# Gathers that wait for a row buffer alone, and inner units moved around the gate products

## The chip, the cores and the metric

The kernel runs on one core of a Trainium2 chip. Its time is the device time of one execution in microseconds (us). Engines are named as in the profile: PE multiplies matrices, PEld loads its weights, DVE works on vectors, ACT evaluates functions, POOL issues the gathers, SP issues most other transfers. Each engine works through its own list of instructions in the order in which the list was built; it waits for semaphores of the others.

## The reference, cut to what matters

One layer of a diffusion transformer over 512 tokens of 2048 numbers: modulation, a retention mixer and an mLSTM mixer, their merge, and then the part that this change touches, a product-key expert layer:

```python
qh = (tb @ w_query).reshape(P_BLOCK, P_HEADS, 2, P_DQ // 2)
s = einsum('thpd,hpkd->thpk', qh, sub_keys)            # 128 + 128 keys per head
sv, si = top_k(s, 16)                                  # per token, head and half
best_s, best_j = top_k(all 16 x 16 sums, 16)           # -> 16 experts of 16384 per head
eid, g = ids of the best, softmax(best_s)
act = gelu(einsum('thkd,td->thk', expert_down[eid], tb))
out = einsum('thk,thkd->td', g * act, expert_up[eid])
```

There are 8 heads, so each token picks 128 expert rows of 2048 numbers, once from expert_down and once from expert_up.

## The kernel before, in words

The kernel computes the expert layer in two ways at once. For 352 of the 512 tokens it is dense: it multiplies all 16384 experts (128 tiles of 128, the inner units, name `hid`) with the tokens, applies Gelu, multiplies with a mostly empty matrix of gates (`gd`, `gt`) and multiplies the result (`hh`) with expert_up (`pac`, `upp`). For the other 160 tokens (128 and 32) it gathers: POOL fetches, for one slot of every token, one row of expert_down or expert_up per partition, 1 MB in all, into a row buffer (`row`). A DVE instruction then forms the scalar product with the token (L1309, function `down`) or adds the weighted row to the result (L1318, function `up`). There are 320 such gathers, 160 of each kind, in a fixed order of slots: slots 0 to 15 of the first 128 belong to head 0, 16 to 31 to head 1, and so on.

Weights arrive as fp32 blocks of 512 KB (`raw`, seven buffers). ACT rounds each to a high part (L228), DVE subtracts to get the low part (L229, called a split here; 770 in all), and PE makes three products of each pair of blocks (L238 to L240). A split pair lives in one of three `ws` buffers, so DVE can be at most three blocks ahead of PE.

The expert layer runs in these stages, told apart here by the count of splits:

- **A, selection** (function `select`): for each of 8 heads PE makes the query products of two halves and the scores (`sc`), and DVE picks the 16 best per half (`top16`, 128-wide), then the 16 best of 256 sums, and finds the ids and gates (`pick`). `pick` of head h writes 16 columns of `eid`. Between the heads PE makes dense tiles that are spilled to memory (`hs`).
- **B, gates** (function `gating`): the selections are transposed, DVE builds one-hot rows (`o`, L1227 to L1231), PE multiplies them (`gp`, L1243) in 88 steps, the results go out in 11 blocks (`gd`). The dense tiles 18 to 55 are spread among these steps: NE_PRE of them ahead, NE_POST behind, the others between.
- **C and D, experts** (function `experts`): for 16 groups of 8 tiles, the second multiplication and the rest of the dense tiles. C is the part up to the 596th split, D the part behind it, up to the closing stage E.

The instructions are written down in the order of the program, and a scheduler of the kernel language then lays them out on each engine: an instruction moves forward to where its inputs and its buffer are free, if the engine has nothing more urgent. The calls `gather(n)` in the dense work spread the 320 slots evenly over stages B to D (SPAN counts the units). A gather, and with it the DVE instruction on its row, is therefore placed by three things: its slot's ids are there, a row buffer is free, and, before the change, the last PE product written ahead of it has been made (`self.last`, `add_manual_dep` in function `rows`). The three row buffers are shared: in stage A one holds the keys (`keys`) and one the selections (`sel`); the third is free once the transposed tokens (`xn`) are done with at the start of A.

Of the kernel before, what the change touches and what calls it, by code (L numbers as in the profile page):

```python
# [12 lines left out]
AF = mybir.ActivationFunctionType  # L13
OP = mybir.AluOpType
AX = mybir.AxisListType
PACE = mybir.DependencyInfo(mybir.DependencyClass.Sync, mybir.DependencyReason.DATA)
PSUM = bass.MemoryType.PSUM
DRAM = bass.MemoryType.DRAM

# [2 lines left out]
KT = D // P  # L22
# [127 lines left out]
X1_BUFS = 5  # L150
NPA = 4
NE_HEAD, NE_SEL = 16, 18
NE_PRE, NE_POST = 1, 2
OT, OB = 8, 2

GX = 32
# [1 line left out]
ND = T - G_  # L158
# [24 lines left out]
class K:  # L183
# [64 lines left out]
    def tjob(self, srcs, targets, nk=KT, order=range(8), one=False):  # L248

        n, last = 0, len(targets) - 1  # L250
        for u, src in enumerate(srcs):
            w = self.weight(src)
            for k8 in order if u else range(8):
                if n == self.LATE:
                    self.flush()
                if n in self.STEPS and self.mixing:
                    next(self.mixing, None)
                c = slice(k8 * P, (k8 + 1) * P)
                for t, (ps, rhs) in enumerate(targets):
                    self.last = self.mm3(ps, (w[:, 0, c], w[:, 1, c]), rhs(u * 8 + k8),  # L260
                                         n == 0 and not (one and t), n == nk - 1 and not (one and t < last))
                n += 1

# [1001 lines left out]
    def spill_steps(self, tiles):  # L1265
        for i in tiles:
            ps = self.ps("hid")
            for u in range(2):
                w = self.weight(self.a["dn"][i, u])
                for k8 in range(8):  # L1270
                    kt = u * 8 + k8
                    c = slice(k8 * P, (k8 + 1) * P)
                    self.last = self.mm3(ps[:, :ND], (w[:, 0, c], w[:, 1, c]), self.HD[kt], kt == 0, kt == KT - 1)
                    if k8 == 7:
                        self.gather(HIDG // 2)
                    if kt < KT - 1:
                        yield
            f = self.d0.tile([P, ND], F32, name="hf", bufs=4)
            self.S.activation(f, ps[:, :ND], AF.Gelu)
            t = self.dp.tile([P, ND], F32, name=f"hs{i}")  # L1280
            self.SY.dma_start(t, f)
            self.HS.append(t)
            yield
# [6 lines left out]
    def gatherer(self):  # L1290

        a, V, S, G, d0 = self.a, self.V, self.S, self.G, self.d0

        dots = [d0.tile([P, n], F32, name=f"dots{n}") for n in (P, GX)]
        wts = [d0.tile([P, n], F32, name=f"wts{n}") for n in (P, GX)]
        eid = [self.eid[0].rearrange("p h k -> p (h k)"), self.eid[1]]
        gacc = [d0.tile([P, D], F32, name=f"gacc{i}", tag=f"h2n{i}") for i in range(2)]
        fold = d0.tile([P, GX], F32, name="fold")
        V.tensor_reduce(fold, self.ident.rearrange("p (q t) -> p t q", t=GX), AX.X, OP.add)

        def rows(src, i, s_):
            r = self.rowbuf([P, D], "row")
            g = G.indirect_dma_start(out=r, out_offset=None, in_=src,  # L1303
                                     in_offset=bass.IndirectOffsetOnAxis(ap=eid[i][:, s_:s_ + 1], axis=0))
            self.tc.add_manual_dep(g.ins, self.last.ins.name, PACE, reason="pace of the gathers")
            return r

        def down(i, s_, r):
            V.scalar_tensor_tensor(r, r, 1.0, self.h2n[i], op0=OP.mult, op1=OP.mult, accum_out=dots[i][:, s_:s_ + 1])  # L1309
            if s_ == dots[i].shape[1] - 1:  # L1310
                S.activation(wts[i], dots[i], AF.Gelu)
                V.tensor_mul(wts[i], wts[i], self.gates[i])

        def up(i, s_, r):
            if s_ == 0:
                V.tensor_scalar(gacc[i], r, wts[i][:, 0:1], None, OP.mult)
            else:
                V.scalar_tensor_tensor(gacc[i], r, wts[i][:, s_:s_ + 1], gacc[i], op0=OP.mult, op1=OP.add)  # L1318

        slots = [(f, w, i, s_) for f, w in ((down, a["dnr"]), (up, a["up"])) for i, n in enumerate((P, GX)) for s_ in range(n)]  # L1320
        NS = len(slots)
        late = []
        done = 0

        def gather(n):

            nonlocal done
            done += n
            while slots and NS - len(slots) < NS * done // SPAN:
                row()  # L1330

        def row():

            if slots:
                f, w, i, s_ = slots.pop(0)
                late.append((f, i, s_, rows(w, i, s_)))
            if len(late) > LAG or not slots:
                f, *x = late.pop(0)
                f(*x)

        self.slots, self.late, self.row, self.gather, self.gacc, self.fold = slots, late, row, gather, gacc, fold

    def experts(self, d2):
        a, V, S, TE, SY, G, d0 = self.a, self.V, self.S, self.TE, self.SY, self.G, self.d0
# [21 lines left out]
        def end0():  # L1366
            nonlocal xg, xh, sqg
            while slots or late:
                row()
            t = d2.tile([P, 2, T], F32, name="xs", tag="gt", bufs=2)  # L1370
            xh, sqg = t[:, 0].rearrange("p (k t) -> p k t", k=KT), t[:, 1]
            xg = self.rowbuf([P, KT, P], "xg")
            SY.dma_start(xg, self.X1[:, :, :P].rearrange("k p t -> p k t"))
            SY.dma_start(xh, self.X1[:, :, P:G_].rearrange("k p t -> p k t"))
# [92 lines left out]
        for g in range(NG):  # L1467
            for i in range(len(hs), min(GRP * (g + 1) + FORE, P)):
                if g == NG - 1 and i % GRP == GRP - 3:
                    end0()  # L1470
                    end1()
                elif g == NG - 1 and i % GRP == GRP - 1:
                    self.todo += [end3, end2]
                hs.append(tile(i))
            hh = hs[GRP * g:GRP * (g + 1)]

            def part(w, q, d_, ps, js):

                own = d_ >= NPA
                for j in js:  # L1480
                    c = slice(j * 256 + d_ % 2 * P, j * 256 + (d_ % 2 + 1) * P)
                    i = 4 * q + j
                    self.last = self.mm3(ps[:, :ND], (w[:, 0, c], w[:, 1, c]), (hh[i][:, 0], hh[i][:, 1]),
                                         i == 0 and (own or g == 0), i == GRP - 1 and (own or g == NG - 1))

            for q in range(GRP // 4):
                ws = [self.weight(a["upt"][g, u, q]) for u in range(NPA // 2)]
                for js in (range(3), (3,)) if g == NG - 1 and q == GRP // 4 - 1 else (range(4),):
                    for d_ in range(NPA):
                        part(ws[d_ // 2], q, d_, pac[d_], js)  # L1490
                gather((UP if (g + 1) * GRP > NE else UP0) * NPA // 2 * 4 // GRP)
            if g == NG - 1:
                for d_ in range(NPA):
                    x2[d_] = d0.tile([P, ND], F32, name="hf", bufs=4)
                    final(d_, pac[d_], xd[:, d_])
            for u in range(8):
                if g == NG - 1 and u in END:
                    (end4, end5)[END.index(u)]()
                if u >= NPA // 2:
                    ds = (2 * u, 2 * u + 1)  # L1500
                    pss = [self.ps("upp") for _ in ds]
                    for q in range(GRP // 4):
                        w = self.weight(a["upt"][g, u, q])
                        for d_, ps in zip(ds, pss):
                            part(w, q, d_, ps, range(4))
                            if q < GRP // 4 - 1:
                                continue
                            if g == 0:
                                V.tensor_copy(x2[d_], ps[:, :ND])
                            elif g < NG - 1:  # L1510
                                V.tensor_add(x2[d_], x2[d_], ps[:, :ND])
                            else:
                                final(d_, ps, x2[d_])
                    gather(UP if (g + 1) * GRP > NE else UP0)
        r = self.r2[:, :ND]
# [18 lines left out]
```

## Time and profile before

Three runs took 4078.6, 4090.9 and 4102.6 us (median 4090.9). The profiled execution took 4096.7 us, its span is 4094.9 us, and its mean granted PE clock 0.981.

| engine | busy us | share | instructions |
|---|---|---|---|
| PE | 3955.3 | 97% | 22470 |
| DVE | 2855.7 | 70% | 4448 |
| ACT | 1325.9 | 32% | 1823 |
| POOL | 500.4 | 12% | 328 |

986 MB are moved, 241 GB/s on the mean. The span is best read by the stages, since DVE and the transfers are at 0.2 to 0.5 of their capacity in the middle of the kernel and at 0.8 to 0.95 in most of its second half, where all the gathers are. In a stretch's row the columns are its length, the busy time of each engine with its count of instructions, the granted PE clock, the busy share of the DMA engines, and GB/s.

### The profile page before, as it was taken

The numbers are of one execution on the slowest core, as the hardware profiler recorded it, in microseconds if no ns is written. First come the engines' busy times: TensorE is split into PE (matmuls) and PEld (weight loads), VectorE is DVE, ScalarE is ACT, GpSimd is POOL, SyncE is SP. The second block draws the span as 40 slices with busy tenths as digits, with TensorE's granted clock in tenths as the row PEclk, the third lists the DMA queues.
The fourth block names the chain that finished last, engine by engine and source line by source line (L and its number), as shares of the span: only waits on it lengthen the run. The fifth ranks groups of instructions, "written<-read, shape, count | busy, mean of one in ns | idle before, by whom it ended". The sixth has DMA issues, their size and how long they took to land.

```text
span 4094.9 us, 56734 instructions
## 1 busy us (share of the span) xinstructions
PE 3955.3 (97%) x22470; PEld 3577.1 (87%) x22470; DVE 2855.7 (70%) x4448; ACT 1325.9 (32%) x1823; POOL 500.4 (12%) x328
## 2 busy tenths in 40 slices
PE   7999999999999999899999998999999999999998
PEld 4788887777788888799989998999999999999998
DVE  7852237677733443488888987888888787888886
ACT  3322124344422222433333333323233332333333
POOL 0000000000000000000001112222222332233320
PEclk7999999999999999999999999999999999999998
DMA  8522237667733444433358898999898898988993
GB/s 298 215 75 85 70 102 256 233 207 245 261 127 112 140 150 149 152 106 109 102 188 303 308 328 342 373 339 371 337 348 342 342 351 326 354 343 345 357 340 102
DMA packets 305723, 986.21 MB, mean 241 GB/s; under 512 B 32944, under 2 KB 106928, under 8 KB 264368
## 3 DMA queue, kind: packets, MB, share of 16 engines
q1 hardware_dynamic: 257072, 642.82, 45.3%
q0 software_dynamic: 46080, 335.56, 21.1%
q10 hardware_dynamic: 2304, 4.20, 0.3%
q8 instruction: 176, 2.88, 0.3%
q14 instruction: 91, 0.75, 0.0%
HBM read 918.87 MB, written 63.57 MB: 240 GB/s over the span
## 4 chain that ended last, share of the span: by engine, by line
PE 56%; DMA 18%; issue 13%; DVE 9%; POOL 2%; ACT 1%; SPq 0%; POOLq 0%; DVEq 0%; ACTq 0%
PE px L240 10%; PE px L239 10%; PE px L238 10%; DMA row<-in_dnr,eid 6%; DMA row<-in_up,eid 6%; DVE ws L229 3%; PE upp L238 2%; PE upp L240 2%; PE upp L239 2%; PE va L238 2%; PE va L239 2%; PE va L240 2%; PE hid L238 2%; PE hid L240 2%; PE hid L239 2%
## 5 line engine op out<-in xcount | busy, mean ns | idle before, releaser
L228 ACT CAST ws<-raw 128x1024 fp32r<-128x1024 f32 x770 | 806.8, 1049 | 1742.2 <-PE px L240 565.3
L229 DVE TENSOR_TENSOR ws<-raw,ws 128x1024 fp32r<-128x1024 f32 x770 | 938.3, 1221 | 563.5 <-ACT ws L228 562.7
L240 PE MATMUL hid<-h,ws 128*128 128x352 f32 x2048 | 662.1, 323 | 24.3 <-DVE ws L229 24.1
L238 PE MATMUL hid<-h,ws 128*128 128x352 f32 x2048 | 677.3, 331 | 0.0
L239 PE MATMUL hid<-h,ws 128*128 128x352 f32 x2048 | 661.8, 323 | 0.0
L1303 POOL DMA_INDIRECT row<-in_dnr,eid x128 | 190.8, 1491 | 2735.1 <-DVE o L1228 2060.1
L238 PE MATMUL upp<-hh,ws 128*128 128x352 f32 x1536 | 500.0, 325 | 0.0
L240 PE MATMUL upp<-hh,ws 128*128 128x352 f32 x1536 | 493.0, 321 | 6.0 <-DVE ws L229 6.0
L239 PE MATMUL upp<-hh,ws 128*128 128x352 f32 x1536 | 494.2, 322 | 0.0
L1309 DVE SCALAR_TENSOR_TENSOR row<-row,h2n 128x2048 f32<-128x2048 f32 x160 | 366.1, 2290 | 123.4 <-DMA row<-in_dnr,eid 97.0
L1318 DVE SCALAR_TENSOR_TENSOR gacc<-row,wts,gacc 128x2048 f32<-128x2048 f32 x158 | 371.2, 2350 | 113.8 <-DMA row<-in_up,eid 95.2
L238 PE MATMUL px<-hhi,ws 128*128 128x512 f32 x1024 | 413.7, 404 | 0.0
L240 PEld LDWEIGHTS hid<-h,ws 128*128 128x128 f32 x2048 | 387.6, 189 | 29.4 <-DVE ws L229 29.1
L240 PE MATMUL px<-hhi,ws 128*128 128x512 f32 x1024 | 408.6, 399 | 0.0
L239 PE MATMUL px<-hlo,ws 128*128 128x512 f32 x1024 | 406.4, 397 | 0.0
L239 PEld LDWEIGHTS hid<-h,ws 128*128 128x128 f32 x2048 | 392.2, 192 | 0.0
L238 PEld LDWEIGHTS hid<-h,ws 128*128 128x128 f32 x2048 | 387.7, 189 | 0.0
L240 PEld LDWEIGHTS upp<-hh,ws 128*128 128x128 f32 x1536 | 289.0, 188 | 7.1 <-DVE ws L229 7.1
L239 PEld LDWEIGHTS upp<-hh,ws 128*128 128x128 f32 x1536 | 292.4, 190 | 0.0
L238 PEld LDWEIGHTS upp<-hh,ws 128*128 128x128 f32 x1536 | 288.6, 188 | 0.0
L1303 POOL DMA_INDIRECT row<-in_up,eid x128 | 207.3, 1619 | 460.1 <-PE hid L240 183.9
L240 PEld LDWEIGHTS px<-hhi,ws 128*128 128x128 f32 x1024 | 192.7, 188 | 48.0 <-issue 2.9
(451 smaller groups left out, 6496.3 us busy)
## 6 DMA issues: line engine op xcount, KB each, us to landing
raw<-in_dn SPq DMA_DIRECT2D x256, 512.0 KB, 5.7
raw<-in_upt SPq DMA_DIRECT2D x256, 512.0 KB, 6.0
raw<-in_wada_r SPq DMA_DIRECT2D x160, 512.0 KB, 4.6
raw<-in_wt SPq DMA_DIRECT2D x130, 512.0 KB, 3.6
gd<-sg SPq DMA_DIRECT2D x11, 2048.0 KB, 13.0
gt<-gd SPq DMA_DIRECT2D x32, 704.0 KB, 7.9
raw<-in_wada_s SPq DMA_DIRECT2D x32, 512.0 KB, 6.0
raw<-in_wn SPq DMA_DIRECT2D x32, 512.0 KB, 3.5
```

Source lines behind the costliest of these rows:

```text
L228: self.S.copy(w[:, 0], r)
L229: self.V.tensor_sub(w[:, 1], r, w[:, 0].bitcast(F32))
L238: mm(out, lhsT=l[0], rhs=r[0], start=start, stop=False)
L239: mm(out, lhsT=l[0], rhs=r[1], start=False, stop=False)
L240: return mm(out, lhsT=l[1], rhs=r[0], start=False, stop=stop)
L1303: g = G.indirect_dma_start(out=r, out_offset=None, in_=src, in_offset=bass.IndirectOffsetOnAxis(ap=eid[i][:, s_:s_ + 1], axis=0))
L1309: V.scalar_tensor_tensor(r, r, 1.0, self.h2n[i], op0=OP.mult, op1=OP.mult, accum_out=dots[i][:, s_:s_ + 1])
L1318: V.scalar_tensor_tensor(gacc[i], r, wts[i][:, s_:s_ + 1], gacc[i], op0=OP.mult, op1=OP.add)
```

## The change

`rows` issues the gather and no longer makes it wait for a PE product. With that the assignments to `self.last`, which served nothing else, and the constant PACE go. NE_PRE goes from 1 to 2 and NE_POST from 2 to 4, so that 32 tiles of inner units instead of 35 lie between the gate products.

```diff
-NE_PRE, NE_POST = 1, 2
+NE_PRE, NE_POST = 2, 4
...
         def rows(src, i, s_):
             r = self.rowbuf([P, D], "row")
-            g = G.indirect_dma_start(out=r, out_offset=None, in_=src,
-                                     in_offset=bass.IndirectOffsetOnAxis(ap=eid[i][:, s_:s_ + 1], axis=0))
-            self.tc.add_manual_dep(g.ins, self.last.ins.name, PACE, reason="pace of the gathers")
+            G.indirect_dma_start(out=r, out_offset=None, in_=src,
+                                 in_offset=bass.IndirectOffsetOnAxis(ap=eid[i][:, s_:s_ + 1], axis=0))
             return r
...
-                    self.last = self.mm3(ps[:, :ND], (w[:, 0, c], w[:, 1, c]), self.HD[kt], kt == 0, kt == KT - 1)
+                    self.mm3(ps[:, :ND], (w[:, 0, c], w[:, 1, c]), self.HD[kt], kt == 0, kt == KT - 1)
```

The change has a second part that the diff doesn't show: without the PE product the scheduler lays the gathers and the instructions on their rows elsewhere. Counted in the built order of DVE, with the splits as the measure of the place:

| stage | splits | row instructions before | after |
|---|---|---|---|
| A | 238 to 297 | 0 | 42 |
| B | 298 to 373 | 41 | 68 |
| C | 374 to 596 | 164 | 210 |
| D | 597 to 759 | 115 | 0 |

The first 40 gathers of the new order all use one row buffer, that of `xn`, and each waits for the DVE instruction on the row before; the next four use two buffers, and all later ones three.

**DVE, stage A, the turn from head 0 to head 1, before.** `sel`, `ef`, `eid` and `ex` end the pick of a head, `ws` is a split, the MAX rows begin the 16 best of the next scores.

```order
1189 L1150 CAST ex<-ef 32x16
1190 L229 TENSOR_TENSOR ws<-raw,ws 128x1024
1191 L1182 MAX sv<-score 128x8 x2
1192 L1183 MAX_INDEX si<-sv,score 128x8 x2
1193 L1184 MATCH_REPLACE score<-sv,score 128x128 x2
```

There the pick is followed by a split and at once by the next head's scores. The same place after; `row,dots` are the products of a gathered row:

```order
1189 L1149 CAST ex<-ef 32x16
1190 L228 TENSOR_TENSOR ws<-raw,ws 128x1024
1191 L1307 SCALAR_TENSOR_TENSOR row,dots_15685<-row,h2n_11758 128x2048 x2
1192 L1181 MAX sv<-score 128x8 x2
1193 L1182 MAX_INDEX si<-sv,score 128x8 x2
1194 L228 TENSOR_TENSOR ws<-raw,ws 128x1024
```

Two row products have come in between, side by side. After, a few rows on, behind two of the four blocks of scores:

```order
1202 L1185 MAX_INDEX si<-sv,score 128x8 x2
1203 L1307 SCALAR_TENSOR_TENSOR row,dots_15685<-row,h2n_11758 128x2048
1204 L228 TENSOR_TENSOR ws<-raw,ws 128x1024
1205 L1307 SCALAR_TENSOR_TENSOR row,dots_15685<-row,h2n_11758 128x2048
1206 L1181 MAX sv<-score 128x8 x2
```

Two more stand here with a split between them. After, the end of the next head's pick:

```order
1251 L1307 SCALAR_TENSOR_TENSOR row,dots_15685<-row,h2n_11758 128x2048
1252 L1145 TENSOR_TENSOR sel<-gt,sm 128x4x16
1253 L1148 SCALAR_TENSOR_TENSOR ef<-sel 128x16
1254 L1148 SCALAR_TENSOR_TENSOR ef<-sel 32x16
1255 L1149 CAST eid<-ef 128x16
1256 L1149 CAST ex<-ef 32x16
1257 L228 TENSOR_TENSOR ws<-raw,ws 128x1024
1258 L1307 SCALAR_TENSOR_TENSOR row,dots_15685<-row,h2n_11758 128x2048 x2
```

So six row products have come into each head, at the same places of every head: two side by side behind the pick, one behind the first two blocks of scores, one a split later, and two in the pick (1243, ahead of the CAST of `bf`, and 1251).

**DVE, stage C, near split 430, before.** `acc` adds a product of the second multiplication.

```order
2137 L1511 TENSOR_TENSOR acc<-acc,upp 128x352
2138 L229 TENSOR_TENSOR ws<-raw,ws 128x1024
2139 L1309 SCALAR_TENSOR_TENSOR row,dots_15685<-row,h2n_11758 128x2048
2140 L229 TENSOR_TENSOR ws<-raw,ws 128x1024
2141 L1511 TENSOR_TENSOR acc<-acc,upp 128x352
2142 L1309 SCALAR_TENSOR_TENSOR row,dots_15685<-row,h2n_11758 128x2048
2143 L1511 TENSOR_TENSOR acc<-acc,upp 128x352
2144 L229 TENSOR_TENSOR ws<-raw,ws 128x1024 x2
```

With three row products to four splits. After:

```order
2203 L1307 SCALAR_TENSOR_TENSOR row,dots_15686<-row,h2n_11759 128x2048
2204 L228 TENSOR_TENSOR ws<-raw,ws 128x1024
2205 L1307 SCALAR_TENSOR_TENSOR row,dots_15686<-row,h2n_11759 128x2048
2206 L228 TENSOR_TENSOR ws<-raw,ws 128x1024
2207 L1509 TENSOR_TENSOR acc<-acc,upp 128x352 x2
2208 L1307 SCALAR_TENSOR_TENSOR row,dots_15686<-row,h2n_11759 128x2048
2209 L228 TENSOR_TENSOR ws<-raw,ws 128x1024
```

Now a row product stands behind every split.

## Rows read from the trace of the kernel before

**Rows 1.** Stretches: stages A, B, C, D and E.

```profile
core 0: us, PE busy (x) PEld busy (x) DVE busy (x) ACT busy (x) POOL busy (x), PEclk, DMA share, GB/s
...
1776.00:2088.00 312.00, 310.65 (x2157) 309.93 (x2156) 259.35 (x881) 102.38 (x124) 0.00 (x0) 1.00 0.36 111
2088.00:2480.00 392.00, 364.48 (x2887) 350.64 (x2886) 323.54 (x394) 145.48 (x208) 64.48 (x41) 0.97 0.86 298
2480.00:3369.80 889.80, 867.69 (x5349) 861.23 (x5348) 747.62 (x791) 279.62 (x339) 241.65 (x165) 0.99 0.92 351
3369.80:4021.00 651.20, 634.35 (x3916) 631.58 (x3915) 529.42 (x456) 202.63 (x249) 189.84 (x115) 0.99 0.88 333
4021.00:4095.00 74.00, 58.77 (x368) 57.97 (x366) 49.28 (x107) 22.36 (x34) 0.00 (x0) 0.90 0.32 100
```

**Rows 2.** The same stretches, DVE's splits (L229) alone.

```profile
1776.00:2088.00 312.00, 72.54 (x60) 1.00 0.36 111
2088.00:2480.00 392.00, 92.69 (x76) 0.97 0.86 298
2480.00:3369.80 889.80, 270.01 (x223) 0.99 0.92 351
3369.80:4021.00 651.20, 197.13 (x163) 0.99 0.88 333
```

**Rows 3.** Waits, 1776 to 2080 us: us in total, times, longest.

```profile
DVE sv L1182 <- ACT score L1115: 38.6, 13, 3.4
...
DVE ws L229 <- ACT ws L228: 12.7, 7, 1.9
```

**Rows 4.** Tile row, 2090 to 2130 us: ns min/median/max, first and last start.

```profile
L1309 DVE SCALAR_TENSOR_TENSOR row<-row,h2n x3: 2291/2291/2292, 2099.0 to 2127.2; 128x2048 f32<-128x2048 f32 x3
L1309 DVE DVE_READ_ACCUMULATOR row<-row,h2n x3: 81/81/83, 2101.2 to 2129.5; 128x1 f32 x3
...
DMA to landing us min/median/max: 5.7/7.8/11.6
```

**Rows 5.** Chain of waits, a gather's release: start us, us, what.

```profile
2428.43 0.04 POOLq L1303
2428.48 0.18 issue
2428.66 2.59 POOL row L1303
```

**Rows 6.** DVE timeline, one head of stage A: start us, us, what.

```profile
1868.49 0.49 DVE L1182 MAX8 sv<-score 128x8 f32<-128x128 f32 x2 [3.41 <-ACT score L1115]
...
1874.12 0.29 DVE L1186 FIND_INDEX8 si<-sv,score 128x8 uint32<-128x128 f32 x1
...
1898.42 0.23 DVE L1132 CAST bf<-bj 128x128 f32<-128x128 uint32 x1
...
1905.49 1.22 DVE L229 TENSOR_TENSOR ws<-raw,ws 128x1024 fp32r<-128x1024 f32 x1
...
1906.75 0.24 DVE L1149 SCALAR_TENSOR_TENSOR ef<-sel 128x16 f32<-128x16 f32 x2
...
1907.27 1.21 DVE L229 TENSOR_TENSOR ws<-raw,ws 128x1024 fp32r<-128x1024 f32 x1
```

**Rows 7.** Waits of PE, 2080 to 2480 us.

```profile
PE pac L238 <- ACT hh L233: 12.7, 1, 12.7
PE gp L1243 <- DVE o L1231: 11.2, 7, 5.3
```

**Rows 8.** Stretches of 10 us in stage B.

```profile
2450.00:2460.00 10.00, 8.14 (x51) 7.86 (x50) 5.08 (x6) 3.87 (x5) 1.87 (x2) 1.00 1.02 418
2460.00:2470.00 10.00, 0.00 (x0) 0.00 (x0) 3.15 (x4) 0.00 (x0) 0.00 (x0) 0.65 1.02 411
2470.00:2480.00 10.00, 8.09 (x36) 7.64 (x37) 6.63 (x12) 3.31 (x6) 0.00 (x0) 0.67 0.60 201
```

**Rows 9.** Tile row, stage C.

```profile
DMA to landing us min/median/max: 5.4/8.8/12.8
```

**Rows 10.** The stretch of 100 us with most transferred.

```profile
3800.00:3900.00 100.00, 98.85 (x618) 98.44 (x617) 86.99 (x72) 32.29 (x42) 29.39 (x19) 1.00 0.94 367
```

More of the change, by code (lines that the diff above doesn't have):

```diff
@@ L15 @@
 AX = mybir.AxisListType
-PACE = mybir.DependencyInfo(mybir.DependencyClass.Sync, mybir.DependencyReason.DATA)
 PSUM = bass.MemoryType.PSUM
@@ L259, in tjob @@
                 for t, (ps, rhs) in enumerate(targets):
-                    self.last = self.mm3(ps, (w[:, 0, c], w[:, 1, c]), rhs(u * 8 + k8),
+                    self.mm3(ps, (w[:, 0, c], w[:, 1, c]), rhs(u * 8 + k8),
                                          n == 0 and not (one and t), n == nk - 1 and not (one and t < last))
@@ L1482, in part @@
                     i = 4 * q + j
-                    self.last = self.mm3(ps[:, :ND], (w[:, 0, c], w[:, 1, c]), (hh[i][:, 0], hh[i][:, 1]),
+                    self.mm3(ps[:, :ND], (w[:, 0, c], w[:, 1, c]), (hh[i][:, 0], hh[i][:, 1]),
                                          i == 0 and (own or g == 0), i == GRP - 1 and (own or g == NG - 1))
```

## The prediction

> **What bounds the kernel now.** I read the stretches by stage first [rows 1]. PE is busy in 310.7 of A's 312 us, 867.7 of C's 889.8 and 634.4 of D's 651.2, so A, C and D run at PE's pace. The reader is to see what is nearly full beside it: DVE at 0.83 in A, 0.83 in B and 0.84 in C, the transfers at 0.36 in A and 0.92 in C. Then the waits: in A DVE is idle for 52.6 us, most of it before the scores [rows 3]; in B PE stands still twice, 5.3 us for the first one-hot rows and 12.7 us for the first `hh` [rows 7], and its clock falls to half in the second gap [rows 8]. The count of splits [rows 2] ties the built orders to these stages.
>
> **The change part by part.** The edit takes one wait from each gather. What decides the time is where the built order then puts the 320 row products, because DVE works in order and every split that PE needs stands in the same list. The table of the change gives 42, 68, 210 and 0 for A to D, where it was 0, 41, 164 and 115. One product costs 2.29 + 0.08 = 2.37 us [rows 4].
>
> *Stage A.* DVE was busy for 259.4 us [rows 1]; 42 products add 99.5, together 359, over the 312 that the stage takes. So DVE becomes the bound here, before any wait is counted. POOL and SP have nothing queued behind a gather that waits; behind a product that waits stand DVE's splits, and PE waits for those. The waits: 40 gathers share one buffer, so a gather starts when the product before it ends, and the next product waits for its landing. From release to POOL's start are 0.04 + 0.18 = 0.2 us [rows 5]; landing takes 5.7 us at the least and 7.8 at the median of a stretch with few gathers [rows 4], which is nearest to A. I take the middle, 6.7, so 6.9 from product to product. The built order gives DVE between two products per head: the rest of the pick and a split, 1906.75 to 1908.48 in rows 6, 1.7 us; nothing; two blocks of scores and a split, 1868.49 to 1874.41, 5.9 us; one split, 1.2 us; then more than 18 us; then the pick from its CAST at 1898.42 to the split at 1905.49 and its end, 8.2 us [rows 6]. The last two cover a landing. The others leave 5.2 + 6.9 + 1.0 + 5.7 = 18.8 us per head, for 40/6 = 6.7 heads 125 us. The sum is 259 + 100 + 125 = 484 us: **+172**. The old idle time is spent inside these waits, since the products stand where DVE waited for scores. Bounds: a landing of 5.4 leaves 13.9 per head, 93 us, +140; one of 7.8, 23.2 and 155 us, +202; if DVE still waits for scores besides, since PE is now late, +52 on that. No wait at all gives +47, which is the floor.
>
> The trace puts a landing at 5.4 us or more [rows 4, 9]. The Trainium skill, page "DMA: Bandwidth & Descriptors", section "Anatomy of one DMA", gives such a transfer from GpSimd a fixed 2 us and its bytes over 436 GB/s, some 4.4 us for 1 MB; by that stage A would cost about +118 in place of +172. No row here is that short, so the trace does not bear it out.
>
> *Stage B.* 27 products more are 64 us; 323.5 + 64 = 388 of 392 us [rows 1]. Here the tiles that NE_PRE and NE_POST move would help PE: its two gaps of 18 us and about 10 us of half clock behind them [rows 7, 8] are what three tiles of 7.8 us (48 products every 0.16 us, the pace of PE in C: 867.7 us over 5349) could fill. But DVE is now full, and a list that is full has little left to be late with; the gaps go and DVE's own length stays. I take 402: **+10**. Bounds: 388, -4; and if half of the old idle 68 us stays, 422, +30.
>
> *Stage C.* 46 products more are 109 us; DVE has 857 of 890 us to work. The transfers: 351 GB/s over 889.8 us are 312 MB, and 46 rows of 1.05 MB make it 361. At 367 GB/s, the most that a stretch of 100 us shows [rows 10], they take 983 us; at the 411 to 418 of a stretch without PE at work [rows 8], 870; at C's own share of 0.92 filled to 1, 946. Three buffers give a gather three places in the order, some 11.4 us less its own 2.4, to land, while the median is already 8.8 and the longest 12.8 [rows 9]; a median of 11 would cost 0.7 us on each of 210 products, 154 us on the 857. I take 965: **+75**, bounds -20 (PE's 868 us) and +150.
>
> *Stage D.* No gather is left: 115 products and 121 MB go. PE is busy for 634.4 of 651.2 us, so at most 17 us and a few of half clock (0.99 [rows 1]) come back: **-20**, bounds 0 and -25. That is the point of the whole change: DVE and the transfers get room in D, where PE is the bound and can use none of it.
>
> *Stage E* has no gathers before or after: 0, the same products in the same order.
>
> The sum is 172 + 10 + 75 - 20 = +237 on the profiled execution's 4096.7 us: 4334. That execution lies 5.8 us above the median of the three runs, so I predict **4328** for a median; the interval follows below.
>
> **The rivals.**
>
> *C stays at PE's pace.* If the transfers keep up with 1.6 MB per split, C costs -20 and the sum is 172 + 10 - 20 - 20 = +142: 4233. For it: 411 GB/s has been seen. Against it: for 20 us alone, around PE's gap, and no stretch of 100 us is above 367; and DVE must do 857 us of work without a wait. The Trainium skill, on the same page, section "Bandwidth", gives 435 GB/s as the ceiling of the fabric and about 358 as a core's share of HBM. By the first this rival is right, by the second C takes 1008 us; C's 351 and the 367 of rows 10 lie by the second.
>
> *Half clock makes A longer.* DVE starves PE in A four times per head. Behind a gap of 12.7 us PE ran at half clock [rows 8]. With PE at half clock throughout, its 311 us of A become 621, more than DVE's 484, and A costs +309: in all 309 + 10 + 75 - 20 = +374, 4465. For it: the waits of 5 to 7 us are frequent. Against it: PE has slack of a third, and three `ws` buffers ahead bridge a part.
>
> *Faster: gathers land before they are needed.* If landings were under 2 us from the release, or the products' places had enough work between them, no wait would be left in A (+47), B would close its gaps for PE (-28), C would shrink to PE's 868 less part of its half clocks (-30), D to -25: -36, 4055. It decides from the point where A's DVE list runs with less than 7 us idle per head. Against it: 5.4 us is the shortest landing, two products stand side by side on one buffer, and B cannot close gaps with DVE at 388.
>
> *The change doesn't do what it says*: the gathers would still be held, by the row buffer, at the old pace, and only the tiles tell: 28 us of PE in B, 4063 at best. Against it speaks the built order: a list that holds 42 products ahead of B is not at the old pace.
>
> **How the numbers follow.** My forecast has 0.6, C at PE's pace 0.2, half clock in A 0.15, faster 0.03, the last 0.02. The range reaches from A and C both at low bounds (140 - 4 - 0 - 25 = +111, about 4200) to A with the old waits and C between (+224 + 30 + 130 = +384, about 4475); I take 4190 to 4470. A measurement of this kernel tells 0.5%, 20 us, from no change (its three runs span 0.6%). Faster by more: 0.03; within: 0.02; slower: 0.95.
>
> **What would show it.** Right: gathers on POOL from about 1790 us on; stage A near 480 us with PE at two thirds and DVE waiting for `row` some 20 us per head; the last `gacc` at split 596, D without a gather and at PE's pace; C with transfers at 0.95 or more. Wrong: A near 312 us, or landings in A under 5 us; C at 870 us with as many products; DVE idle in B as much as before.

## The result, and the profile after

The changed kernel takes 4300.6 us (median of 6 runs, 4296.84 to 4307.45); the kernel before took 4093.9 us beside it (median of 6). The ratio is 1.0506, with a 95% interval of 1.0482 to 1.0531: slower by 207 us. The forecast was 4328 us. The profiled execution of the changed kernel has a span of 4301.9 us; its granted clock is 0.964 on the mean.

First the page of the changed kernel's profile, in 40 slices of 107.5 us (counted from 0; 9 is 90% or more): the busy tenths of POOL, of the transfers, and the granted clock of PE.

```profile
POOL 0000000000000000011112222333334331000000
...
PEclk7999999999999999888889998999999999999999
DMA  8522248677633444344459999999999998444453
```

The gathers (POOL) fill a tenth or more of a slice from slice 17 on (the first, at 1779.55 us, lies in slice 16) and end in slice 33. The transfers are at 0.9 or more from slice 21 to slice 32 and at about half behind slice 33. PE's clock is below 0.9 in slices 16 to 20, which is stage A, and in slice 24, around the end of B.

The stages of the changed kernel, cut at the same splits as [rows 1], to about one split of some 4 us; the columns are those of [rows 1].

```profile
1774.00:2245.00 471.00, 346.25 (x2150) 339.87 (x2149) 348.26 (x955) 102.12 (x124) 53.80 (x44) 0.86 0.51 170
2245.00:2653.00 408.00, 370.03 (x2898) 354.33 (x2897) 381.27 (x459) 146.10 (x210) 101.65 (x68) 0.95 0.98 357
2653.00:3604.50 951.50, 892.66 (x5352) 869.43 (x5351) 856.56 (x767) 279.01 (x337) 345.41 (x208) 0.98 0.98 378
3604.50:4228.40 623.90, 623.90 (x3906) 623.88 (x3905) 280.05 (x340) 205.25 (x247) 0.00 (x0) 1.00 0.49 153
4228.40:4302.00 73.60, 58.40 (x368) 57.76 (x366) 49.41 (x108) 22.50 (x34) 0.00 (x0) 0.92 0.33 101
```

| stage | before | forecast | after | difference | difference forecast |
|---|---|---|---|---|---|
| A | 312.0 | 484 | 471.0 | +159.0 | +172 |
| B | 392.0 | 402 | 408.0 | +16.0 | +10 |
| C | 889.8 | 965 | 951.5 | +61.7 | +75 |
| D | 651.2 | 631 | 623.9 | -27.3 | -20 |
| E | 74.0 | 74 | 73.6 | -0.4 | 0 |

What lies ahead of A is 2 us shorter; 209 less 2 are the 207 us between the two spans. PE is busy in all of D, in 893 of C's 951.5 us and in only 346 of A's 471.

Stage A of the changed kernel, the waits from 1774 to 2245 us (us in total, times, longest): the answers to [rows 3].

```profile
POOL row L1302 <- PE px L239: 1738.8, 1, 1738.8
...
DVE row L1307 <- DMA row<-in_dnr,eid: 120.6, 22, 7.5
PE hid L239 <- DVE ws L228: 119.2, 21, 9.8
```

DVE works for 348.3 us and waits 120.6 us for rows: together 468.9 of the 471. So DVE's list is the stage, and PE stands still for 119.2 us because its split is late. The waits for the scores that led [rows 3] are gone from DVE's waits: that time is spent inside the waits for rows. The first line only says that the first gather waits for the start of A.

One head of DVE in stage A of the changed kernel, which answers to [rows 6]: start us, us, what, and in brackets the idle time ahead of it and what ended it.

```profile
1844.02 2.26 DVE L1307 SCALAR_TENSOR_TENSOR row<-row,h2n 128x2048 f32<-128x2048 f32 x1
...
1846.76 1.21 DVE L228 TENSOR_TENSOR ws<-raw,ws 128x1024 fp32r<-128x1024 f32 x1
...
1852.20 2.29 DVE L1307 SCALAR_TENSOR_TENSOR row<-row,h2n 128x2048 f32<-128x2048 f32 x1 [4.24 <-DMA row<-in_dnr,eid]
...
1860.55 2.29 DVE L1307 SCALAR_TENSOR_TENSOR row<-row,h2n 128x2048 f32<-128x2048 f32 x1 [6.05 <-DMA row<-in_dnr,eid]
...
1868.63 2.29 DVE L1307 SCALAR_TENSOR_TENSOR row<-row,h2n 128x2048 f32<-128x2048 f32 x1
1870.85 1.22 DVE L228 TENSOR_TENSOR ws<-raw,ws 128x1024 fp32r<-128x1024 f32 x1
...
1879.28 2.29 DVE L1307 SCALAR_TENSOR_TENSOR row<-row,h2n 128x2048 f32<-128x2048 f32 x1 [7.20 <-DMA row<-in_dnr,eid]
```

The waits are 4.24, 6.05, 0 and 7.20 us, 17.5 in sum, where the prediction had 18.8 per head. The covered place is the product at 1868.63: the scores stand ahead of it. The landing, from the row of the tile in the same stage (least, median, most), was 5.7 us where the prediction took 6.7:

```profile
DMA to landing us min/median/max: 5.4/5.7/8.4
```

What such a wait does to PE, in stretches of 4 us of the changed kernel's stage A (columns of [rows 1]):

```profile
1856.00:1860.00 4.00, 0.00 (x0) 0.00 (x0) 0.00 (x0) 0.54 (x1) 0.00 (x0) 0.97 0.81 262
1860.00:1864.00 4.00, 0.00 (x0) 0.00 (x0) 3.45 (x9) 0.00 (x0) 0.88 (x1) 0.50 0.00 0
1864.00:1868.00 4.00, 3.05 (x10) 3.05 (x11) 4.00 (x23) 0.00 (x0) 0.06 (x1) 0.50 0.80 268
1868.00:1872.00 4.00, 3.35 (x15) 3.06 (x14) 4.00 (x8) 0.94 (x1) 0.80 (x1) 0.75 0.31 125
```

PE stands still for some 9 us, its granted clock falls to 0.50 (1.2 GHz) in the gap, and PE takes up work again at half clock. The same follows each of the 14 gaps, two per head and 6.5 to 9.8 us long, in which PE waits for a split in A. That is the 36 us by which PE is busy longer in A than in [rows 1] with as many matmuls.

### The profile page after: what moved, and what is told of

Its sections match the earlier page's. It is cut to its first block, busy times and chain, and to the rows that moved or that the text cites. A ratio compares the mean times of both kernels' runs of the same rounds, so it can differ in the third digit from the quotient of the medians.

```text
span 4301.9 us, 56787 instructions
## 1 busy us (share of the span) xinstructions
PE 4009.6 (93%) x22470; PEld 3610.0 (84%) x22470; DVE 2862.4 (67%) x4448; ACT 1328.5 (31%) x1823; POOL 505.3 (12%) x328
## 4 chain that ended last, share of the span: by engine, by line
PE 53%; issue 16%; DMA 12%; DVE 11%; POOL 4%; ACT 1%; SPq 0%; DVEq 0%; POOLq 0%; ACTq 0%
PE px L239 8%; PE px L237 8%; PE px L238 8%; DMA row<-in_up,eid 6%; POOL row L1302 4%; PE hid L237 3%; PE hid L238 3%; PE hid L239 3%; PE upp L237 2%; PE upp L238 2%; DVE gacc L1316 2%; PE upp L239 2%; DMA row<-in_dnr,eid 2%; DVE ws L228 2%; PE va L238 2%
## 5 line engine op out<-in xcount | busy, mean ns | idle before, releaser
L239 PE MATMUL hid<-h,ws 128*128 128x352 f32 x2048 | 679.9, 332 | 143.4 <-DVE ws L228 143.0
L237 PE MATMUL hid<-h,ws 128*128 128x352 f32 x2048 | 688.3, 336 | 0.0
L238 PE MATMUL hid<-h,ws 128*128 128x352 f32 x2048 | 674.0, 329 | 0.0
L239 PEld LDWEIGHTS hid<-h,ws 128*128 128x128 f32 x2048 | 399.1, 195 | 156.8 <-DVE ws L228 156.0
L1302 POOL DMA_INDIRECT row<-in_dnr,eid x128 | 180.0, 1406 | 2519.3 <-PE px L239 1738.8
L238 PEld LDWEIGHTS hid<-h,ws 128*128 128x128 f32 x2048 | 402.4, 196 | 0.0
L237 PEld LDWEIGHTS hid<-h,ws 128*128 128x128 f32 x2048 | 398.7, 195 | 0.0
```

The source lines that it names most:

```text
L237: mm(out, lhsT=l[0], rhs=r[0], start=start, stop=False)
L238: mm(out, lhsT=l[0], rhs=r[1], start=False, stop=False)
L239: return mm(out, lhsT=l[1], rhs=r[0], start=False, stop=stop)
L1302: G.indirect_dma_start(out=r, out_offset=None, in_=src, in_offset=bass.IndirectOffsetOnAxis(ap=eid[i][:, s_:s_ + 1], axis=0))
```

## The experiments

Each is an edit of the kernel before or of the changed kernel; ratios are to the kernel before, run beside it on the same chip. Lengths of stages without a row are cut at DVE's splits, by which before has A to D of 311.0, 391.8, 892.4 and 644.6 us, and the changed kernel 470.9, 405.7, 953.2 and 620.0. Each length is that of one execution: D took 635.8 to 644.6 us in the four kernels that have 115 row products there, so a difference of less than some 9 us in one stage says little.

**The tiles alone** (on the kernel before):

```
-NE_PRE, NE_POST = 1, 2
+NE_PRE, NE_POST = 2, 4
```

> Gathers paced as before, only NE_PRE and NE_POST at 2 and 4. Theory (the cost of the change lies in where the row products went; the tiles only fill gaps of TensorE): stage B loses its two gaps of 5.3 and 12.7 us and some half clock, 392 us become about 370, A, C and D stay: about 4072 us. Rival (the tiles cost by making the gate steps denser on VectorE): stage B grows to 395 to 410 us, 4095 to 4110 us.

Measured: 1.0017 (0.9999 to 1.0034), so the theory fell and the rival held. PE's waits in stage B of this kernel:

```profile
PE gp L1243 <- DVE o L1231: 26.0, 11, 7.4
...
PE pac L238 <- ACT hh L233: 10.0, 1, 10.0
```

The gap ahead of the first `hh` shrank by 2.7 us against [rows 7], the wait for the one-hot rows grew from 11.2 to 26.0. B is 403.5 us, 12 us longer than before.

**The freed gathers alone** (on the changed kernel):

```
-NE_PRE, NE_POST = 2, 4
+NE_PRE, NE_POST = 1, 2
```

> Gathers free as in the changed kernel, NE_PRE and NE_POST at 1 and 2. The built order has 42, 72, 206 and 0 row products in A to D. Theory: A as in the changed kernel (472 us), C and D too, and B some 0 to 20 us longer, since VectorE is full there in either case: 4300 to 4320 us. Rival (the tiles have a share in the loss): 4290 us or less.

Measured: 1.0506 (1.0472 to 1.0540), the changed kernel's own ratio. The loss is the gathers' alone; the tiles move B by 7 us (412.9 against 405.7), within the spread of a stage, and the time not at all.

**Free gathers, but none in A** (on the changed kernel):

```
...
+if src is a["dnr"]:
+    self.gate = self.gate or self.last
+    self.tc.add_manual_dep(g.ins, self.gate.ins.name, PACE, ...)
```

Every gather of expert_down waits for the one product that was the last ahead of the first gather in the program's text, and for no later one. The built order has 0, 66, 211 and 43 row products in A to D.

> As the changed kernel, but the 160 gathers of expert_down also wait for the product that stands ahead of the first gather, early in stage B, so none can be laid into A. The built order has 0, 66, 211 and 43 row products in A to D. Theory (A costs by products and by landings on one buffer that nothing hides; the same rows cost little where three buffers are free and TensorE is the bound): A back to 312 us (-160), B and C as in the changed kernel (408, 953), D 43 products longer in reach of the transfers, +10: about 4150 us. Rival (the moved work is the same wherever it stands, the 100 us of products and their waits come back in D): 4230 to 4260 us.

Measured: 1.0162 (1.0130 to 1.0194). Its stages A and C:

```profile
1771.80:2083.80 312.00, 310.64 (x2156) 309.93 (x2155) 258.87 (x881) 102.64 (x124) 0.00 (x0) 1.00 0.36 111
...
2492.50:3450.50 958.00, 895.51 (x5365) 875.16 (x5363) 855.33 (x812) 277.55 (x337) 343.08 (x211) 0.98 0.96 375
```

A is back at 312.0 us, the length of before to the tenth; C keeps its loss. So the two losses are separate, and A's goes with the 42 products that stand in it. The time came 17 us above the 4150 expected, mostly in C and in D, where 43 gathers remain.

**Only the 42 gathers of A free** (on the kernel before, with 2 and 4 tiles):

```
+if src is not a["dnr"] or i or s_ >= 42:
     self.tc.add_manual_dep(g.ins, self.last.ins.name, PACE, ...)
```

> As the kernel before with NE_PRE and NE_POST at 2 and 4, but the first 42 gathers are free of the pace. The built order has 42, 0, 163 and 115 row products in A to D. Theory: A as in the changed kernel, +160 us; B without any row product about 360 us (-30); C and D as before: about 4225 us. Rival (the loss lies in the transfers of C and B, A's products hide beside TensorE): 4070 to 4120 us.

Measured: 1.0352 (1.0319 to 1.0385). Its stages A, B and C:

```profile
1771.50:2240.20 468.70, 346.80 (x2151) 340.32 (x2150) 348.18 (x955) 101.99 (x124) 50.93 (x42) 0.87 0.49 168
2240.20:2613.70 373.50, 363.78 (x2888) 351.03 (x2887) 241.27 (x323) 145.41 (x209) 0.00 (x0) 0.98 0.64 199
2613.70:3508.50 894.80, 868.19 (x5353) 860.48 (x5352) 746.02 (x787) 279.39 (x338) 254.38 (x164) 0.99 0.91 347
```

A is within 2.3 us of the changed kernel's, C within 5 of that of before. The rival fell; 4243.3 us is 18 us above the theory's 4225. The parts of the two kernels, 3.5% and 1.6%, add up to the change's 5.1%. Without any row product in B (the built order has 0 there), that stage is 18.5 us shorter than before.

**The same with 1 and 2 tiles:**

```
-NE_PRE, NE_POST = 2, 4
+NE_PRE, NE_POST = 1, 2
```

> The kernel before with the first 42 gathers free, as in the run with stage A's part alone, but with NE_PRE and NE_POST left at 1 and 2; B holds no row products. That run's B was 373 us. Theory (row products on DVE are what lengthens B, the number of tiles ahead is not): B 371 to 378, time within 0.2% of that run's 4243. Rival (the tiles help once DVE has room, and the old numbers leave PE's gaps of 18 us open): B 385 to 392, time 4255 to 4262.

Measured: 1.0349 (1.0316 to 1.0381), 4241.7 us, within 0.04% of the kernel with 2 and 4 tiles. Its B is 381.0 us:

```profile
2244.50:2625.50 381.00, 363.96 (x2890) 351.56 (x2889) 241.40 (x324) 145.85 (x209) 0.00 (x0) 0.97 0.63 195
```

That lies between the ranges of theory and rival, 11 us below before's 392.0 and 7.5 us above the B of the kernel with 2 and 4 tiles. The 7.5 us lie within the spread of a stage: in D, where the two kernels have the same work, these two executions differ by 6.2 us (642.0 and 635.8). The time shows none of them.

**Half products in A** (on the changed kernel):

```
+n = D // 2 if i == 0 and s_ < 42 else D
-V.scalar_tensor_tensor(r, r, 1.0, self.h2n[i], ...)
+V.scalar_tensor_tensor(r[:, :n], r[:, :n], 1.0, self.h2n[i][:, :n], ...)
```

> The changed kernel with the first 42 products of rows made over 1024 of the 2048 numbers (half of each of these scalar products is left out); the gathers stay whole. The built order has 43, 66, 211 and 0 products in A to D. Theory (in A products and landings stand one behind the other in VectorE's list, on one buffer): each of the 42 saves some 1.1 us of the whole, A goes from 471 to about 425 us and the sum from 4301 to about 4255 us. Rival (A is held by TensorE at half clock, VectorE has room): A stays at 460 to 471 us.

Measured: 1.0385 (1.0356 to 1.0414). Stage A, and DVE's wait in it:

```profile
1785.50:2221.20 435.70, 344.88 (x2158) 338.70 (x2157) 305.96 (x961) 102.61 (x124) 60.07 (x44) 0.89 0.54 184
```

```profile
DVE row L1308 <- DMA row<-in_dnr,eid: 129.4, 21, 7.4
```

DVE has 42 us less to do and A is 35 us shorter, with PE busy for as long as without the edit. So PE's half clock does not set A's length; DVE's list does. 9 us went into longer waits, which is most of why it was not the 46 expected.

**Half of each `up` on DVE** (on the changed kernel):

```
+h = slice(0, D // 2)
-V.scalar_tensor_tensor(gacc[i], r, wts..., gacc[i], ...)
+V.scalar_tensor_tensor(gacc[i][:, h], r[:, h], wts..., gacc[i][:, h], ...)
```

> The changed kernel with the accumulation of every expert_up row but the first of each group made over 1024 of the 2048 numbers (half of the result is left out); the gathers stay whole. It takes some 1.1 us of VectorE's work from each of 158 instructions, 175 us in all, nearly all in stage C; the built order ends the gathers at split 566 in place of 595. Theory (C is bound by transfers, whose engines are at 0.98): the same bytes take the same time, C and D together lose 10 to 30 us: about 4280 us. Rival (C is bound by VectorE, 858 of 953 us busy): C and D together lose 70 us or more, 4230 us or less.

Measured: 1.0619 (1.0589 to 1.0649), outside both expectations. Stage C (cut at the same split as above), and two stretches of 100 us in it:

```profile
2657.50:3655.00 997.50, 906.86 (x5339) 891.80 (x5337) 695.64 (x768) 276.22 (x335) 307.11 (x208) 0.95 0.93 362
...
3400.00:3500.00 100.00, 88.29 (x516) 86.85 (x515) 67.46 (x68) 25.04 (x28) 38.56 (x28) 0.95 1.00 399
...
3600.00:3700.00 100.00, 100.00 (x627) 100.00 (x626) 42.55 (x50) 34.01 (x42) 0.00 (x0) 1.00 0.47 152
```

DVE has 161 us less to do in C, and C is longer. Shorter DVE instructions let the scheduler place the last one at split 566 in place of 595: the same gathers in fewer tiles. In the first stretch the transfers are full and PE is busy for 88 of 100 us; in the second no gather is left and PE is alone. Up to the last row product C takes 887 us in place of 948, and behind it 110 in place of 3. My expectations had counted the time that the transfers save and left out that PE's own pace follows for some 30 splits more behind the last gather.

**Half of each `up` row fetched** (on the changed kernel, DVE's work kept):

```
-G.indirect_dma_start(out=r, out_offset=None, in_=src, ...)
+n = D if src is a["dnr"] else D // 2
+G.indirect_dma_start(out=r[:, :n], out_offset=None,
+    in_=src if n == D else src.rearrange("e (t d) -> (e t) d", t=2), ...)
...
```

The accumulation reads these 1024 numbers twice. The built order is that of the changed kernel.

> The changed kernel, except that each gather of expert_up fetches 1024 numbers per row in place of 2048 (the output is not the reference's: the second half of a row is a copy of the first); DVE still works on 2048 numbers per row, in the same order as in the changed kernel. In stage C 160 of the 210 gathers are such, 84 MB less, 277 MB in all. Theory (the transfers bound C, not DVE's list): at the 378 GB/s of the changed kernel's C these take 733 us, so PE's 868 us or DVE's 857 bound it, C falls from 951.5 to 870 to 900, and the time to 4220 to 4250. Rival (DVE works in order, and PE's splits stand behind products however fast the rows come): C stays above 930, the time at 4280 to 4300.

Measured: 1.0357 (1.0329 to 1.0385), 4246.1 us. Stage C and, of it, one stretch of 100 us:

```profile
2659.50:3548.00 888.50, 869.78 (x5354) 863.40 (x5354) 849.79 (x765) 280.97 (x337) 372.77 (x208) 0.99 0.86 310
...
3100.00:3200.00 100.00, 100.00 (x627) 100.00 (x626) 98.32 (x75) 34.24 (x42) 48.22 (x27) 1.00 0.83 286
```

C falls from 951.5 to 888.5 us, PE's pace, with the same 208 gathers and the same order. In the second row DVE is busy for 98.3 of 100 us and PE still never waits. So DVE's work was not what bound C; what went with the bytes was. In C of the changed kernel DVE waits 62 us for rows, here 15:

```profile
DVE gacc L1316 <- DMA row<-in_up,eid: 39.2, 48, 3.5
```

```profile
DVE gacc L1319 <- DMA row<-in_up,eid: 7.7, 4, 5.7
```

The first line is of the changed kernel, the second of this run; the rest of the 62 and 15 us are waits for the other rows. The theory held; the rival (above 930) fell. Half rows take time from the transfers and shorten the waits for landings at once, and no kernel with more row buffers was run, so the two are told apart only by the share of 0.98 in the changed kernel's C, which leaves the transfers little room.

**Two attempts to keep the good side.** Each gather waits for the product noted at the gather ahead of it, one step earlier (on the kernel before; the first gather waits for its own):

```
+self.paces.append(self.last)
-self.tc.add_manual_dep(g.ins, self.last.ins.name, PACE, ...)
+self.tc.add_manual_dep(g.ins, self.paces[-2].ins.name, PACE, ...)
```

> The kernel before, with each gather waiting for the product at which the gather ahead of it was paced, so it may start one gather earlier; NE_PRE and NE_POST at 1 and 2. The built order has 0, 42, 164 and 114 products. Theory (the pace is needed to keep gathers out of A and spread over B to D, but it starts each a little late): VectorE's 200 us of waits for rows shrink, and of TensorE's 65 us idle in B to D some 20 to 30 go: 4065 to 4080 us. Rival (TensorE's gaps have other causes, or transfers start earlier and collide): 4090 to 4105 us.

Measured: 1.0017 (1.0000 to 1.0033). The theory fell: in C and D DVE still waits 87.8 us for rows of expert_up and 41.9 us for those of expert_down (of the first 128 tokens), where it was 95.2 and 45.9. POOL also waits for PE's products nearly as long as before, 1123 us for 1160, so the step started the gathers hardly earlier; whether the pace starts them late is not shown. With fewer gathers in B besides (`HIDG` 14 to 6, 20 products there):

> As v1_lag1, and with HIDG at 6 in place of 14, so that 20 products of rows in place of 42 stand in B, 177 in C and 123 in D. Theory (VectorE bounds B: without any row product B took 373 us, with 41 some 392 to 404): B loses about 10 us, C and D have TensorE as the bound and take the 22 rows for 5 us: 4060 to 4075 us. Rival (each row costs the same in C and D): as v1_lag1.

Measured: 1.0052 (1.0034 to 1.0070). B fell by 9 us to 382.9, and C, with 13 products more, rose by 32 to 924.6: C pays more than B gives back.

**Products in A's covered places alone** (on the kernel before): 14 gathers, paced by the spilled tiles of A, two per head; the other 306 are spread over B to D.

```
+j = s_ if src is a["dnr"] and i == 0 else NS
-self.tc.add_manual_dep(g.ins, self.last.ins.name, PACE, ...)
+self.tc.add_manual_dep(g.ins, (self.marks[2 + j] if j < 14 else self.last).ins.name, PACE, ...)
...
```

> The kernel before (NE_PRE and NE_POST at 1 and 2, gathers paced), but the first 14 gathers are paced by the products of the spilled tiles in A, two for each of the last seven heads. The built order puts them at two of the six places of the changed kernel, in the pick, where 18 and 8 us of other work stand ahead of each; B, C and D have 39, 157 and 110 products. Theory (in A a product costs only where a landing isn't covered, and VectorE's 33 us for 14 products fit its 52 us of idle time): A stays within 311 to 320 us, B to D lose 5 to 15 us: 4085 to 4100 us, where the kernel before has 4098. Rival (any product in A costs in full, since the scores wait behind it): A 340 us or more, 4115 to 4130 us.

Measured: 1.0054 (1.0038 to 1.0071). Its stages A and B:

```profile
1778.70:2090.50 311.80, 309.69 (x2152) 309.41 (x2151) 285.12 (x899) 102.40 (x124) 16.31 (x14) 1.00 0.49 158
2090.50:2495.70 405.20, 366.84 (x2890) 353.09 (x2889) 322.04 (x400) 145.34 (x208) 60.86 (x39) 0.96 0.83 284
```

A does not grow, 311.8 us, though 14 products stand in it and DVE is busy for 26 us more than in [rows 1]: the theory held for A. It fell for the rest: C and D did not gain from rows done early (897.3 and 641.5 us), B came out 13 us longer than in [rows 1] with two products fewer in it, and the time, 4117.4 us, lies above the 4100 expected. No kernel that ran was faster than the kernel before; the tiles alone and the pace one step earlier, both at 1.0017, can hardly be told from it.

## Why the prediction was right, point by point

**Stage A** was the largest term, and its mechanism is shown from three sides: without the 42 products A is 312.0 us, with them alone 468.7, and with half of their work 435.7. The sum of DVE's work and its waits was 259 + 100 + 125 = 484 and measured 348.3 + 120.6 = 469. The work came out 11 us lower than my 359, the waits 4 lower. The waits came near in part by cancelling: at three of the four places in the head shown they were 0.9 to 1.0 us shorter (landing 5.7 where I took 6.7), at the fourth 1.5 longer, where the gather began during a split. PE starved twice per head where I had four times: two waits of DVE in a row make one gap of PE. The covered places that I took from [rows 6] are real: two products per head left A at 311.8. By the Trainium skill, page "DMA: Bandwidth & Descriptors", section "Anatomy of one DMA", a landing would have been an estimated 4.4 us and A +118. The shortest landing of the changed kernel's A is 5.4 and A grew by 159, so the trace does not agree with it.

**Stage B**: +16 where I had +10, within its bounds. The step that failed is the one on the tiles: I priced what they could fill at 28 us and held that the gaps go and a full DVE swallows the gain. The gap ahead of the first `hh` did not go: it is 14.8 us in the changed kernel, 12.7 before. Alone, with DVE as free as before, the tiles gave nothing (1.0017); with no products in B the two B differ by 7.5 us, within the spread, and the times not at all. Of the 16 us, 12 are longer waits of PE in B: 10.6 us for splits (2.5 before) and 21.1 for `hh` (13.7), against 7.9 for one-hot rows (11.2). Among the kernels run, B is 373 and 380 us without a product in it, 383 with 20, 392 to 405 with 39 to 42 and 403 to 413 with 66 to 72: it rises with the products. The transfers are also fuller, 0.98 against 0.86, and no run here separates the two. The kernels with 39 to 42 products differ by 13 us in B as PE's wait for one-hot rows does: 11.2 us in the kernel before, 14.4 with the pace one step earlier, 26.0 with the tiles alone and 23.7 with products in A. What makes DVE late with these rows stays open.

**Stage C**: +62 where I had +75. The transfers are its bound, as I had it: 0.98 of full, and PE's pace comes back when 84 MB go. The amount was right (951.5 us at 378 GB/s are 360 MB, 361 forecast); the rate was 378 GB/s where [rows 10] had 367 as the most. The nearest of my three estimates was C's own share filled to 1, 946 us. The one from 411 to 418 GB/s rested on a misreading: PE was at work in one of those two stretches, for 8.14 of 10 us [rows 8]. The other price that I gave, 154 us of landings on 210 products, was too high: DVE waits 62 us for rows in C, and the median landing there is 9.4 us where I took 11. The rival that C stays at PE's pace needed the transfers to keep up, and they did not. The Trainium skill, page "DMA: Bandwidth & Descriptors", section "Bandwidth", gives about 358 GB/s as a core's share of HBM, when both cores of a pair stream, and 435 as the fabric's ceiling. The 951.5 us at 378, and 399 over 100 us, lie between the two, so neither figure alone gives C's length.

**Stage D**: -27 where I had -20 and a bound of -25. PE is busy in all of its 623.9 us. The 2 us beyond the bound lie in the cut, since D before holds one split more in the table: cut at the same splits D fell by 24.6 us, from 644.6 to 620.0.

**Half clock in A**, the rival at 4465: PE did run at half clock behind each gap, but its busy time rose from 311 to 346 us only. It has 125 us of idle time left in A, and A followed DVE's work when the 42 products were halved. **Faster** (4055) needed landings of under 2 us or less than 7 us of idle DVE per head; 17.5 were measured in the head shown. **The change doing nothing** is refuted by POOL's first gather, at 1779.55 us.

The forecast was 13 us too long in A, 13 in C and 7 in D, and 6 too short in B: together about the 27 us by which it lies above the median. That C came within 14 us is partly luck, since 965 was a choice among estimates from 870 to 1011 (857 of work and 154 of landings). The sum for the low end of the range has C at 0 where C's own low bound is -20; with that it would be about 4180, which changes nothing here.

## What to carry to other kernels

A dependency that looks like a needless wait can be what keeps a scheduler from moving work forward into an engine whose list is already nearly full (DVE at 0.83 in A): before it is removed, count in the built order what moves into each stage, and add its time to what that engine does there. An instruction that waits for a transfer in an in-order list costs everyone behind it its whole landing, less the work that stands between it and the release; look for the places with such work, since the two products per head that stood there cost stage A nothing. And spread transfers over all stretches that another engine bounds: the same bytes in fewer tiles made C bound by bytes while D had no use for the room.

## What the runs showed of the hardware that was not expected

The same gather instruction took 0.94 us on POOL or up to 1.95, by what DVE was doing when it began. Below (POOL in stage A of the changed kernel) the first began 0.2 us ahead of a split, the one at 1846.76 in the head shown above; the second while DVE stood still; the third 0.35 us behind the start of the split at 1870.85. The second is followed by its product 5.8 us later, at 1860.55; the third by its product 8.1 us later, at 1879.28.

```profile
1846.56 0.94 POOL L1302 DMA_INDIRECT row<-in_dnr,eid  x1 [8.53 <-DVE ef L1148]
...
1854.77 0.94 POOL L1302 DMA_INDIRECT row<-in_dnr,eid  x1 [7.28 <-DVE row L1307]
...
1871.20 1.68 POOL L1302 DMA_INDIRECT row<-in_dnr,eid  x1 [7.15 <-DVE row L1307]
```

So it matters which comes first. Of the 44 gathers in A, 29 began with no instruction running on DVE that reads two tiles of SBUF, and took 0.94 us, though such an instruction began beside 20 of them. The other 15 began while one ran, a split or the product `oh` of the pick, and 14 of them took what was left of it, 0.87 or 1.13 us, and 0.81 us more. In C of the changed kernel, where DVE is busy for 0.90 of the time and 189 of 208 gathers began during a split, the 128 of expert_up for the first 128 tokens took 1.68 us on the mean. The Trainium skill, page "SBUF — State Buffer", section "Who interferes with whom", says that a DVE instruction with two inputs from SBUF contends with a GpSimd instruction that reads SBUF; the split has two such inputs, and the trace agrees where the split came first; where it came second the gather took no longer. The 0.7 us do not explain all of the 2.3 us to the product; the rest was not tested.

The transfers of one core held 390 GB/s and more over 100 us at a share of 1.00:

```profile
3200.00:3300.00 100.00, 97.53 (x590) 93.84 (x589) 94.00 (x71) 27.68 (x33) 41.92 (x25) 1.00 1.00 394
3300.00:3400.00 100.00, 92.66 (x556) 89.96 (x555) 91.00 (x70) 29.00 (x35) 39.50 (x24) 0.98 1.00 390
```

The kernel before, whose best such stretch moved 367 GB/s at 0.94 [rows 10], never filled them over 100 us. So the 367 was no bound. Nor has a full share one rate: in B of the changed kernel a stretch at 1.00 moved 357 GB/s, with DVE busy throughout.

```profile
2400.00:2500.00 100.00, 98.83 (x820) 94.42 (x820) 100.00 (x122) 40.36 (x58) 23.83 (x16) 1.00 1.00 357
```
